# Adding the attention mask on VectorE in nine of twelve groups, with other steps and orders re-assigned, in a two-layer attention trunk

## The chip, the cores and the metric

The kernel runs on one core of a Trainium2 chip. The metric is the time of one execution on the device in microseconds (us); the median of the runs shown is compared. In the text PE is TensorE (matmuls and transposes, with PEld for its weight loads), DVE is VectorE, ACT is ScalarE, POOL is GpSimd, SP is the engine whose queue issues the DMAs. L353 is line 353 of the kernel before; the change moves most lines of the changed kernel one to twelve further down, so that its names are given where its lines are meant.

## The reference, cut to what matters

Two layers over 256 tokens of width 1024, 16 heads of 64. Layer 0 attends over a sliding window of 128 tokens with a learned sink a head, in 2 key heads; layer 1 is block-sparse attention which, at 256 tokens and a block of 256, is plain causal attention, in 4 key heads. Both gate the attention output by silu(z) and add an output projection to the residual; a last RMSNorm ends the trunk.

```python
for i in range(DEPTH):                       # DEPTH = 2
    hn = rmsnorm(h, norm_g[i])
    q, k, v, z = split_proj(hn, w_in, n_kv)  # one input projection
    q, k = apply_rope(q, cos, sin), apply_rope(k, cos, sin)
    # layer 0: softmax over [masked scores (128-token window), sink]
    # layer 1: softmax over causal scores
    o = attention(q, k, v)
    h = h + (o.reshape(B, S, MIX_WIDTH) * silu(z)) @ w_out[i]
return rmsnorm(h, final_g)
```

The mask is additive, 0 or -1e30, and the softmax subtracts the row's maximum (in layer 0 the larger of it and the sink) before the exponential.

## The kernel before, in words

**Weights.** Each layer's weights come from HBM in pieces of 128 x 1024 float32 (`load`). A piece is used in one of two ways. Most are split (`split`, L100 to L120): ACT writes a rounded high part `whi` (L113), DVE subtracts it from the piece to get the low part `wlo` (L114), and every block of the projection is then three matmuls, high by high, high by low and low by high (L150 to L152 with the activations' own halves, the `quad` tiles; L438 to L440 and L475 to L477 in the output projections). In the text such three matmuls are a triple. The pieces numbered in `NATIVE` are not split: one full float32 matmul of `xf` (L148), which the profile records as two matmuls. `PACE` makes the ACT part of each split wait for the DVE part of the split before it.

**Attention.** `attn(c, b, u, qs)` handles one group of heads for one block `b` of 128 queries. There are six groups a layer, called here (layer, c, b, u): for b = 0 one group of 8 heads over 128 keys, for b = 1 two groups (u = 0, 1) of 4 heads over 256 keys. A group goes as follows:

- PE: scores into the one tile `sc` in PSUM (`NSC` = 1), two banks, one for the even and one for the odd heads (L349); then two bf16 matmuls, one a bank, add the mask, an identity times the mask repeated for every head of the bank (L353; 512 columns, or 256 in layer 1 for b = 1, where half of the keys need no mask).
- DVE: one reduction over all 1024 score columns gives the negated maximum of each head, `nm` (L355); in layer 0 `nm` is then taken against the sink (L359) and `es` prepared (L360).
- ACT: an exponential a head from `sc` into `p`, with its sum in `rs` (L363); in layer 0 the sink's exponential `es` (L361), which DVE adds to `rs` (L365).
- DVE: the reciprocal `ri` (L366); then a scaling of `p` a head, by ACT (L369) for groups in the table `PSC`, else by DVE (L371).
- PE: eight transposes (L377) into two `tr` tiles; each copied to a `pT` tile (`NPT` of them) by DVE (L380) for groups in `PEV`, else by ACT (L382).
- PE: the product with the values into `o` (L392); DVE multiplies by the gate `sz` (L398), ACT takes the high part (L404), POOL (groups in `GLP`) or DVE the low part (L405).

**Other work that tables place.** `RPL`: which rotary halves (L242, L243) go to POOL instead of DVE. `SZP`: which gate tiles (L423 to L426) go to POOL. `SQP`: which squares of the residual for the norm go to POOL (L175) instead of ACT (L177). `NACC`: into how many tiles the squares are summed; the norm's sum over the partitions is then one matmul a tile and token block (L189).

**Order.** PE is fed by a scheduler that orders the instructions of each engine at build time from the priorities `PRI0` and `PRI1` and its own estimate of times; on the chip each engine then runs its list strictly in that order. `ORDERS` sets in which order the three groups of a half c come. Between the scores and the transposes of a group other matmuls (projections, earlier groups) are placed, so that the softmax of the group can run meanwhile on DVE and ACT.

**End.** `outp_r(1, True)` makes the last rows, 128 tokens at a time (t = 0, 1): matmuls, the residual add (L479), the sum of squares by ACT for the first 512 columns (L483) and by a two-input multiply-and-reduce on DVE for the rest (L486), the power on POOL (L492), and the scaling by norm and weight: POOL multiplies two of the four quarters by the weight ahead (L489) and ACT scales them (L495), DVE does the other two in one step each (L496). For t = 1 each of the four quarters is one DMA (L500).

Of the kernel before, what the change touches and what calls it, by code (L numbers as in the profile page):

```python
# [26 lines left out]
PSC = [(0, 0, 0, 0), (0, 0, 0, 1), (0, 0, 1, 1), (0, 1, 0, 1), (1, 0, 1, 0), (1, 0, 1, 1), (1, 1, 0, 0), (1, 1, 1, 0)]
PEV = [(0, 0, 0, 0), (0, 0, 1, 0), (0, 1, 0, 0), (0, 1, 0, 1), (0, 1, 1, 0), (0, 1, 1, 1), (1, 0, 0, 0), (1, 0, 1, 0), (1, 1, 0, 0), (1, 1, 0, 1), (1, 1, 1, 0)]
NRAW, NHI, NLO = 10, 7, 5
PRI0 = {'xf': -162.8, 'hi': -265.1, 'sr': -286.8, 'tr': -272.9, 'skv': 98.1, 'st': -212.1, 'kv': -263.2, 'sq0': 99.4, 'q0': 98.9, 'sz0': 45.8, 'z0': 45.7, 'a0': -114.0, 'sq1': -459.0, 'q1': -26.7, 'a1': -421.4, 'sz1': -118.7, 'z1': 71.8, 'so0': -61.1, 'o0': -294.2, 'so1': 9.0, 'o1': -290.0, 'r0': -69.2, 'r1': -190.1, 'rk': -186.0, 'p0': -402.1, 'p1': -134.3, 'e0': 48.7, 'e1': -109.7, 'f0': -206.4, 'f1': 27.1}  # L30
# [14 lines left out]
def trunk(ctx: ExitStack, tc: tile.TileContext, xT, gf, sinks, consts, masks, wkva, w, out):  # L45
# [161 lines left out]
    for layer in range(2):  # L207
# [122 lines left out]
        def attn(c, b, u, qs):  # L330
# [31 lines left out]
            for n in range(nh):  # L362
                nc.scalar.activation(p[:, n], sc[:, n % 2, n // 2], AF.Exp, bias=nm[:, n:n + 1], accum_out=rs[:, n:n + 1])  # L363
# [226 lines left out]
```

## Time and profile before

| | |
|---|---|
| three runs | 222.77, 222.79, 223.54 us, median 222.79 |
| the profiled execution's own time | 223.15 us |
| its span, first to last instruction | 221.3 us |
| granted TensorE clock, mean | 0.989 |
| PE busy | 212.5 us, 1535 matmuls |
| DVE busy | 157.6 us |
| ACT busy | 128.7 us |
| POOL busy | 63.5 us |

How to read it: the span is 1.85 us shorter than the profiled execution's time, and that execution is 0.36 us over the median. The end of a matmul is modelled in the profile, so that overlapping matmuls in a row show as one unbroken stretch; how long one takes out of PE's stream is read from the distance between starts. In a row of the timeline a group of equal instructions is merged, with the start of the first, the time to the end of the last, and their number behind the x.

### The profile page before, as it was taken

What the parts mean: (1) busy time and instruction counts of PE and PEld (TensorE: products, weight loads), DVE (VectorE), ACT (ScalarE), POOL (GpSimd) and SP (SyncE); (2) the same over time, 40 slices, a digit from 0 to 9 for tenths busy, and PEclk for the clock granted to TensorE, in tenths of its full rate; (3) what the DMA queues carried; (4) which work ended last, traced back from release to release, by engine and by line L of the source; (5) the groups of instructions that cost most, each with busy time, mean ns of one, the idle gap of its engine ahead of it and who ended that gap; (6) DMA issues with size and microseconds to landing.
All of it is one profiled execution on the core that took longest, in us unless ns stands there. A gap on an engine that the chain in (4) does not pass through costs nothing.

```text
span 221.3 us, 4120 instructions
## 1 busy us (share of the span) xinstructions
PE 212.5 (96%) x1535; PEld 185.9 (84%) x1535; DVE 157.6 (71%) x291; ACT 128.7 (58%) x323; POOL 63.5 (29%) x69
## 2 busy tenths in 40 slices
PE   8989999999999999999999999999999999999970
PEld 4879999986989778989999999999799987668870
DVE  2458767858777769958975586889637799577471
ACT  7593355785469445327971555383967985843121
POOL 2562960220241712013631362320620011011231
PEclk9999999999999999999999999999999999999995
DMA  5899998535152323354534476654410000000022
GB/s 172 280 400 412 405 392 288 167 143 169 44 170 77 115 64 129 95 175 123 172 115 142 156 244 182 186 193 129 114 76 3 1 4 0 0 0 3 0 95 95
DMA packets 10532, 31.71 MB, mean 143 GB/s; under 512 B 1296, under 2 KB 2704, under 8 KB 10512
## 3 DMA queue, kind: packets, MB, share of 16 engines
q1 hardware_dynamic: 10512, 31.45, 42.7%
q8 instruction: 12, 0.20, 0.4%
q14 instruction: 8, 0.07, 0.1%
HBM read 30.39 MB, written 1.05 MB: 142 GB/s over the span
## 4 chain that ended last, share of the span: by engine, by line
PE 88%; ACT 3%; DMA 3%; SPq 2%; DVE 1%; issue 1%; POOL 0%; POOLq 0%; ACTq 0%
PE mm L152 12%; PE mm L151 11%; PE mm L150 11%; PE mm L148 9%; PE sc L349 6%; PE o L392 6%; PE tr L377 5%; PE mm L438 4%; PE mm L439 4%; PE mm L440 3%; PE mm L477 3%; PE mm L475 3%; PE mm L476 3%; DMA hg<-xT 3%; PE sc L353 3%; SPq L95 1%
## 5 line engine op out<-in xcount | busy, mean ns | idle before, releaser
L114 DVE TENSOR_TENSOR wlo<-wraw,whi 128x1024 fp32r<-128x1024 f32 (+2 forms) x48 | 60.2, 1257 | 19.3 <-ACT whi L113 15.0
L113 ACT ACTIVATE whi<-wraw 128x1024 fp32r<-128x1024 f32 (+2 forms) x48 | 48.7, 1025 | 40.2 <-DVE wlo L114 29.9
L150 PE MATMUL mm<-quad,whi 128*128 128x256 f32 x216 | 64.0, 298 | 0.1
L152 PE MATMUL mm<-quad,wlo 128*128 128x256 f32 x216 | 62.0, 289 | 0.1
L151 PE MATMUL mm<-quad,whi 128*128 128x256 f32 x216 | 61.5, 286 | 0.0
L150 PEld LDWEIGHTS mm<-quad,whi 128*128 128x128 f32 x216 | 41.3, 192 | 1.1 <-ACT whi L113 0.6
L151 PEld LDWEIGHTS mm<-quad,whi 128*128 128x128 f32 x216 | 41.4, 191 | 1.0 <-issue 0.4
L152 PEld LDWEIGHTS mm<-quad,wlo 128*128 128x128 f32 x216 | 41.0, 191 | 0.8 <-DVE wlo L114 0.3
L363 ACT ACTIVATE p<-sc,nm 128x128 f32<-128x128 f32 (+1 forms) x64 | 26.0, 425 | 15.9 <-DVE nm L359 9.1
L148 PE MATMUL mm<-xf,wraw 128*128 128x256 f32 x112 | 26.9, 380 | 0.7 <-ACT xf L168 0.7
L148 PEld LDWEIGHTS mm<-xf,wraw 128*128 128x128 f32 x112 | 20.2, 190 | 3.4 <-ACT xf L168 1.1
L423 POOL TENSOR_TENSOR th<-th,z 128x256 f32<-128x256 f32 x9 | 8.7, 967 | 42.8 <-ACT th L421 42.6
L355 DVE TENSOR_REDUCE nm<-sc 128x4 f32<-128x1024 f32 (+1 forms) x12 | 14.6, 1220 | 7.2 <-PE sc L353 7.2
L242 POOL TENSOR_TENSOR t<-t,csr 128x512 f32<-128x512 f32 (+1 forms) x7 | 11.4, 1624 | 26.0 <-DVE t L238 18.9
L405 POOL TENSOR_TENSOR quad<-gf,quad 128x256 fp32r<-128x256 f32 x7 | 5.2, 742 | 46.5 <-ACT quad L404 46.5
L438 PE MATMUL mm<-quad,whi 128*128 128x256 f32 x64 | 18.3, 291 | 0.0
L439 PE MATMUL mm<-quad,whi 128*128 128x256 f32 x64 | 18.2, 285 | 0.0
L440 PE MATMUL mm<-quad,wlo 128*128 128x256 f32 x64 | 18.0, 282 | 0.0
L170 DVE SCALAR_TENSOR_TENSOR quad<-hg,quad 128x256 fp32r<-128x256 f32 x16 | 11.1, 702 | 7.1 <-ACT quad L169 7.1
L349 PE MATMUL sc<-ks,qs 64*128 64x128 f32 (+1 forms) x128 | 15.2, 348 | 0.0
L377 PE MATMUL tr<-cst,p 128*128 128x128 f32 x96 | 14.6, 275 | 0.0
L180 POOL TENSOR_TENSOR sq<-sq 128x256 f32<-128x256 f32 x14 | 11.9, 849 | 6.8 <-ACT sq L177 6.0
(105 smaller groups left out, 387.8 us busy)
## 6 DMA issues: line engine op xcount, KB each, us to landing
wraw<-w SPq DMA_DIRECT2D x50, 512.0 KB, 4.8
wraw<-wkva SPq DMA_DIRECT2D x2, 512.0 KB, 8.6
wraw<-w SPq DMA_DIRECT2D x3, 256.0 KB, 4.2
hg<-xT SPq DMA_DIRECT2D x2, 256.0 KB, 6.4
wraw<-gf SPq DMA_DIRECT2D x1, 512.0 KB, 3.5
out<-of SPq DMA_DIRECT2D x2, 256.0 KB, 2.2
out<-of SPq DMA_DIRECT2D x4, 128.0 KB, 1.9
hg<-xT SPq DMA_DIRECT2D x3, 128.0 KB, 3.5
```

Source lines behind the costliest of these rows:

```text
L113: ia = nc.scalar.activation(a[:, c0:c1], r[:, c0:c1], AF.Copy)
L114: ib = nc.vector.tensor_sub(b[:, c0:c1], r[:, c0:c1], a[:, c0:c1].bitcast(F32))
L148: nc.tensor.matmul(ps, wh, x, start=start, stop=stop)
L150: nc.tensor.matmul(ps, wh, xh, start=start, stop=False)
L151: nc.tensor.matmul(ps, wh, xl, start=False, stop=False)
L152: nc.tensor.matmul(ps, wl, xh, start=False, stop=stop)
L349: nc.tensor.matmul(sc[:, par, i], qs[half, 2 * us[0] + i, b * P:(b + 1) * P], ks[half, (h0 + n) // per, :nk], start=i == 0, stop=False)
L363: nc.scalar.activation(p[:, n], sc[:, n % 2, n // 2], AF.Exp, bias=nm[:, n:n + 1], accum_out=rs[:, n:n + 1])
L377: nc.tensor.transpose(pt[:, n], p[:, n0 + n, kt * P:(kt + 1) * P], ident)
L438: nc.tensor.matmul(ps, wh, gh, start=k == 0, stop=False)
L439: nc.tensor.matmul(ps, wh, gl, start=False, stop=False)
L440: nc.tensor.matmul(ps, wl, gh, start=False, stop=k == 3)
```

## The change

1. Nine of the twelve groups, those in the new table `TTM`, get no mask matmuls. For each of their heads one DVE instruction reads the scores from PSUM and the mask from SBUF, adds them, writes the negated sum to `p` and reduces it with a minimum to `nm`. In layer 0 it starts from the negated sink, so that L359 falls away. It replaces the reduction over the whole group; the instruction is followed by a short one that writes its accumulator out. The exponential then reads `p` instead of `sc` and takes the scale -1, and in these groups `sc` is free after DVE's last head instead of after ACT's. The three groups left as they were are (0, 0, 0, 0), (1, 0, 1, 0) and (1, 1, 1, 0).
2. The last rows: POOL multiplies the first 512 columns by the weight in one step while the second 512 are still in work; ACT scales that half in one instruction, DVE the other half in one, and each half is one DMA, for t = 1 too.
3. Tables: pieces 9 and 17 are split instead of native and piece 10 native instead of split; layer 0 runs two rotary halves more on DVE; scaling moves from DVE to ACT in three groups of four heads; the copies of three groups of layer 0 move from DVE to ACT, and of one group of layer 1, on balance, to DVE; three more squares go to POOL; the squares are summed in two tiles a layer instead of one; six `pT` tiles instead of three; a different order of groups in layer 0, and all priorities.

```diff
-NATIVE = (1, 2, 5, 6, 9, 13, 17, 31)
-RPL = [(0, 'k'), (0, 0, 0), (0, 0, 1), (0, 1, 1), (1, 'k'), (1, 0, 0), (1, 1, 0)]
+NATIVE = (1, 2, 5, 6, 10, 13, 31)
+RPL = [(0, 'k'), (0, 0, 0), (1, 'k'), (1, 0, 0), (1, 1, 0)]
...
-PSC = [(0, 0, 0, 0), (0, 0, 0, 1), (0, 0, 1, 1), (0, 1, 0, 1), (1, 0, 1, 0), (1, 0, 1, 1), (1, 1, 0, 0), (1, 1, 1, 0)]
+PSC = [(0, 0, 0, 0), (0, 0, 0, 1), (0, 0, 1, 0), (0, 0, 1, 1), (0, 1, 1, 1), (1, 0, 1, 0), (1, 0, 1, 1), (1, 1, 0, 0), (1, 1, 1, 0), (1, 1, 1, 1)]
...
-NRAW, NHI, NLO = 10, 7, 5
+NRAW, NHI, NLO = 10, 6, 5
-NPT = 3
+NPT = 6
-ORDERS = [[[(0, 0), (1, 0), (1, 1)], [(0, 0), (1, 0), (1, 1)]], [[(0, 0), (1, 1), (1, 0)], [(0, 0), (1, 1), (1, 0)]]]
+ORDERS = [[[(1, 0), (0, 0), (1, 1)], [(1, 0), (0, 0), (1, 1)]], [[(0, 0), (1, 1), (1, 0)], [(0, 0), (1, 1), (1, 0)]]]
+TTM = [(0, 0, 1, 0), (0, 0, 1, 1), (0, 1, 0, 0), (0, 1, 1, 0), (0, 1, 1, 1), (1, 0, 0, 0), (1, 0, 1, 1), (1, 1, 0, 0), (1, 1, 1, 1)]
-SQP = [(0, 0), (0, 2), (0, 4), (1, 0)]
-NACC = [1, 1]
+SQP = [(0, 0), (0, 1), (0, 3), (0, 5), (1, 1), (1, 5), (1, 6)]
+NACC = [2, 2]
...
+            wide = (layer, c, b, u) in TTM
             for n in range(nh):
...
                 nc.tensor.matmul(sc[:, par, i], qs[half, 2 * us[0] + i, b * P:(b + 1) * P],
-                                 ks[half, (h0 + n) // per, :nk], start=i == 0, stop=False)
-            k0 = nk - P if layer else 0
-            for par in range(2):
-                nc.tensor.matmul(sc[:, par, :, k0:], mkb[:, 0], mask[:, None, k0:].to_broadcast([P, np_, nk - k0]),
-                                 start=False, stop=True)
-            nc.vector.tensor_reduce(nm.rearrange("p (i r) -> p r i", r=2), sc, axis=mybir.AxisListType.X, op=OP.max,
-                                    negate=True)
+                                 ks[half, (h0 + n) // per, :nk], start=i == 0, stop=wide and i == np_ - 1)
+            if wide:
+                for n in range(nh):
+                    nc.vector.tensor_tensor_reduce(out=p[:, n], in0=sc[:, n % 2, n // 2], in1=mask, scale=-1.0,
+                                                   scalar=3.0e38 if layer else nsink[:, h0 + n:h0 + n + 1],
+                                                   op0=OP.add, op1=OP.min, accum_out=nm[:, n:n + 1])
+            else:
...
             for n in range(nh):
-                nc.scalar.activation(p[:, n], sc[:, n % 2, n // 2], AF.Exp, bias=nm[:, n:n + 1], accum_out=rs[:, n:n + 1])
+                if wide:
+                    nc.scalar.activation(p[:, n], p[:, n], AF.Exp, bias=nm[:, n:n + 1], scale=-1.0, accum_out=rs[:, n:n + 1])
+                else:
+                    nc.scalar.activation(p[:, n], sc[:, n % 2, n // 2], AF.Exp, bias=nm[:, n:n + 1], accum_out=rs[:, n:n + 1])
...
-                            if c0 % 512 == 0:
-                                nc.gpsimd.tensor_mul(hf[:, c0 // 512], hv[:, :2], gk[:, c0 // P:c0 // P + 2])
+                            if c0 == 0:
+                                nc.gpsimd.tensor_mul(hf, hv, gk[:, :4])
...
+                        nc.scalar.activation(o[:, :4], hf, AF.Copy, scale=ms[:, 1:])
+                        nc.vector.scalar_tensor_tensor(o[:, 4:], h[:, 4:, tok], ms[:, 1:], gk[:, 4:], op0=OP.mult, op1=OP.mult)
                         for i in range(2):
-                            nc.scalar.activation(o[:, 4 * i:4 * i + 2], hf[:, i], AF.Copy, scale=ms[:, 1:])
-                            nc.vector.scalar_tensor_tensor(o[:, 4 * i + 2:4 * i + 4], h[:, 4 * i + 2:4 * i + 4, tok],
-                                                           ms[:, 1:], gk[:, 4 * i + 2:4 * i + 4], op0=OP.mult, op1=OP.mult)
-                            for j in (range(2) if t else (0,)):
-                                k0, k1 = (4 * i + 2 * j, 4 * i + 2 * j + 2) if t else (4 * i, 4 * i + 4)
-                                nc.sync.dma_start(out[tok, k0 * P:k1 * P], o[:, k0:k1].rearrange("p k s -> p (k s)"))
+                            nc.sync.dma_start(out[tok, 512 * i:512 * i + 512],
+                                              o[:, 4 * i:4 * i + 4].rearrange("p k s -> p (k s)"))
```

What the tables do to the order is shown at one place on two engines, the group (0, 1, 1, 0): second half of layer 0, second query block, first four heads. The rows are of the lists that each engine runs; `mm`, `sc`, `tr` and `o` are PSUM tiles, `quad` and `xf` activations, a row with x8 is eight equal instructions, and a native matmul (of `xf`), a score or a product `o` counts once where the profile records two.

PE before, from the scores of that group to the next matmuls behind them:

```order
321 L349 MATMUL sc<-ks,qs 128x256 x4
322 L353 LDWEIGHTS mkb
323 L353 MATMUL sc<-mkb 128x512
324 L353 LDWEIGHTS mkb
325 L353 MATMUL sc<-mkb 128x512
326 L377 MATMUL tr<-cst,p 128x128 x8
327 L438 MATMUL mm<-quad,whi 128x256
```

PE now, from the same scores on (the transposes in row 248 are those of the group ahead, (0, 0, 1, 1)):

```order
244 L351 MATMUL sc<-ks,qs 128x256 x4
245 L404 MATMUL o<-pT,vs 64x256 x4
246 L153 MATMUL mm<-quad,wlo 128x256
247 L149 MATMUL mm<-xf,wraw 128x256 x3
248 L389 MATMUL tr<-cst,p 128x128 x8
249 L149 MATMUL mm<-xf,wraw 128x256
250 L151 MATMUL mm<-quad,whi 128x256
```

The two mask matmuls and their weight loads are gone, and the group stands earlier, inside the gate projection. Before, its own transposes come in row 362, between them 8 transposes, 27 matmuls of triples, 4 native ones, 8 products `o` and 4 heads of the next scores with their masks. Now they begin in row 267, behind the rows shown, five more matmuls of triples, the eight heads of scores of (0, 1, 0, 0) in row 256 and ten matmuls of triples.

DVE before, from the reduction of that group to its neighbours' work:

```order
79 L355 TENSOR_REDUCE nm<-sc 128x2x2
80 L380 COPY pT<-tr 128x512
81 L359 TENSOR_TENSOR nm<-nm,nsink 128x4
82 L360 TENSOR_TENSOR es<-nm,sink 128x4
83 L380 COPY pT<-tr 128x512
84 L398 TENSOR_TENSOR gf<-o,sz 128x256
85 L365 TENSOR_TENSOR rs<-rs,es 128x4
86 L366 RECIPROCAL ri<-rs 128x4
```

DVE now, from the last of the four heads (an instruction of the reduce kind is listed as ISA, its accumulator's read in the row behind it) to the scaling:

```order
80 L355 ISA p,nm<-sc,mkb,nsink 128x256
81 L355 ISA nm 128x1
82 L115 TENSOR_TENSOR wlo<-wraw,whi 128x1024
83 L369 TENSOR_TENSOR es<-nm,sink 128x4
84 L432 TENSOR_TENSOR z<-mm,rh 128x256
85 L377 TENSOR_TENSOR rs<-rs,es 128x4
86 L378 RECIPROCAL ri<-rs 128x4
87 L383 TENSOR_SCALAR p<-p,ri 128x256 x4
```

Four pairs (rows 74 to 81) stand where one reduction and L359 stood, with nothing between them, and a weight split now lies between them and the group's `es`. On ACT the four exponentials, then the next split's `whi`, then the `es` of this group follow each other.

More of the change, by code (lines that the diff above doesn't have):

```diff
@@ L349, in attn @@
                 nc.tensor.matmul(sc[:, par, i], qs[half, 2 * us[0] + i, b * P:(b + 1) * P],
-                                 ks[half, (h0 + n) // per, :nk], start=i == 0, stop=False)
-            k0 = nk - P if layer else 0
-            for par in range(2):
-                nc.tensor.matmul(sc[:, par, :, k0:], mkb[:, 0], mask[:, None, k0:].to_broadcast([P, np_, nk - k0]),
-                                 start=False, stop=True)
-            nc.vector.tensor_reduce(nm.rearrange("p (i r) -> p r i", r=2), sc, axis=mybir.AxisListType.X, op=OP.max,
-                                    negate=True)
+                                 ks[half, (h0 + n) // per, :nk], start=i == 0, stop=wide and i == np_ - 1)
[5 more added lines that the diff above has]
+            else:
+                k0 = nk - P if layer else 0
+                for par in range(2):
+                    nc.tensor.matmul(sc[:, par, :, k0:], mkb[:, 0], mask[:, None, k0:].to_broadcast([P, np_, nk - k0]),
+                                     start=False, stop=True)
+                nc.vector.tensor_reduce(nm.rearrange("p (i r) -> p r i", r=2), sc, axis=mybir.AxisListType.X, op=OP.max,
+                                        negate=True)
             if layer == 0:
                 es = work.tile([P, 8], F32, name="es", bufs=4)[:, :nh]
-                nc.vector.tensor_tensor(nm, nm, nsink[:, h0:h0 + nh], op=OP.min)
+                if not wide:
+                    nc.vector.tensor_tensor(nm, nm, nsink[:, h0:h0 + nh], op=OP.min)
                 nc.vector.tensor_add(es, nm, sink[:, h0:h0 + nh])
@@ L467, in outp_r @@
                     if final:
-                        hf = act.tile([P, 2, 2, P], F32, name="hf", tag="quad", bufs=6)
+                        hf = act.tile([P, 4, P], F32, name="hf", tag="quad", bufs=6)
                         gk = gfin.rearrange("p (k s) -> p k s", s=P)
```

10 lines of the change are left out of this document (5 added, 5 removed).

## The prediction

> **What bounds the kernel now.** I read the page first: busy times, then the shares of the chain that ended last.
>
> ```profile
> span 221.3 us, 4120 instructions
> PE 212.5 (96%) x1535; PEld 185.9 (84%) x1535; DVE 157.6 (71%) x291; ACT 128.7 (58%) x323; POOL 63.5 (29%) x69
> ...
> PE 88%; ACT 3%; DMA 3%; SPq 2%; DVE 1%; issue 1%; POOL 0%; POOLq 0%; ACTq 0%
> ```
>
> PE is on the chain for 88% of the span. Whether DVE has room for more work has to be read by stage, so the second view is the busy time by stretches (columns: stretch, its length, then PE, PEld, DVE, ACT and POOL).
>
> ```profile
> 16.20:88.00 71.80, 71.68 (x522) 61.70 (x523) 54.85 (x117) 41.47 (x120) 23.34 (x22) 1.00 0.57 201
> 120.00:200.00 80.00, 80.00 (x614) 69.90 (x613) 60.15 (x97) 52.70 (x133) 19.53 (x17) 1.00 0.30 93
> 215.00:221.30 6.30, 0.00 (x0) 0.00 (x0) 1.70 (x7) 0.91 (x2) 0.56 (x1) 0.62 0.25 83
> ```
>
> The first two hold the attention of layer 0 and of layer 1. PE has no free time there, at a granted clock of 1.00; DVE is busy 76% and 75%, ACT 58% and 66%. So what leaves PE's stream shortens the kernel, and what is added to DVE costs nothing as long as PE does not come to wait for it. The last stretch is PE-free: 6.3 us of norm, scaling and output, all on the path.
>
> **The PE terms.** Mask matmuls first, by the distance of starts in PE's timeline: the wide pair of layer 1's first group, the narrow pair, and scores with no mask behind them (half a group, followed by other work).
>
> ```profile
> 135.72 0.39 PE L152 MATMUL mm<-quad,wlo 128*128 128x256 f32 x1
> 135.94 0.28 PE L150 MATMUL mm<-quad,whi 128*128 128x256 f32 x1
> ...
> 141.59 0.60 PE L353 MATMUL sc<-mkb 128*128 128x512 bf16 x2
> 142.16 0.28 PE L150 MATMUL mm<-quad,whi 128*128 128x256 f32 x1
> 142.28 0.28 PE L151 MATMUL mm<-quad,whi 128*128 128x256 f32 x1
> ...
> 150.74 0.39 PE L353 MATMUL sc<-mkb 128*128 128x256 bf16 x2
> 151.09 0.28 PE L150 MATMUL mm<-quad,whi 128*128 128x256 f32 x1
> ```
>
> Without masks the second matmul behind the scores starts 0.22 us after the first. With a wide pair it starts 0.57 after the pair's start, with a narrow one 0.35. The pairs cost 0.35 and 0.13. Seven of the nine groups have wide pairs (five of layer 0, two of 8 heads in layer 1), two have narrow ones: 7 x 0.35 + 2 x 0.13 = 2.7 us less. The chain books more on them, which is my upper end:
>
> ```profile
> 36.23 1.73 PE mm L148 x8
> 62.69 1.09 PE sc L349 x16
> 73.99 0.87 PE tr L377 x8
> 76.29 1.01 PE o L392 x8
> 120.51 0.34 PE tr L189 x4
> 141.66 0.54 PE sc L353 x2
> 150.81 0.33 PE sc L353 x2
> ```
>
> By its 0.54 and 0.33 it is 7 x 0.54 + 2 x 0.33 = 4.4 us. I take 2.7, because the chain counts to modelled ends and starts are recorded.
>
> One native piece fewer: 8 full matmuls are 16 records, two rows like the 1.73, 3.46 us; as triples they are 24 x 0.12 (142.16 to 142.28) = 2.88 us. 0.6 us less. Squares summed in two tiles: 8 more of L189, at 0.34 / 4 = 0.085, 0.7 us more. PE in sum: -2.7 - 0.6 + 0.7 = -2.6 us. The instructions that only change their place on PE keep their cost.
>
> **What DVE and ACT get.** The rows of the groups by line and shape (busy us, mean ns, idle before); of the multiply-and-reduce kind before has only three, in the last rows.
>
> ```profile
> L114 DVE TENSOR_TENSOR wlo<-wraw,whi 128x1024 fp32r<-128x1024 f32 x45 | 58.8, 1306 | 18.7 <-ACT whi L113 14.4 <-PE mm L152 3.0 <-PE mm L440 0.9
> L113 ACT ACTIVATE whi<-wraw 128x1024 fp32r<-128x1024 f32 x45 | 47.3, 1062 | 40.0 <-DVE wlo L114 29.9 <-DMA wraw<-w 4.0 <-PE tr L377 2.2
> L380 DVE COPY pT<-tr 128x512 f32<-128x512 f32 x18 | 12.0, 683 | 1.9 <-PE o L392 1.9
> L355 DVE TENSOR_REDUCE nm<-sc 128x4 f32<-128x1024 f32 x8 | 9.8, 1222 | 6.5 <-PE sc L353 6.5
> L420 DVE TENSOR_TENSOR z<-mm,rh 128x256 f32<-128x256 f32 x16 | 6.5, 414 | 0.9 <-PE mm L152 0.6 <-PE mm L148 0.3
> L371 DVE TENSOR_SCALAR p<-p,ri 128x256 f32<-128x256 f32 x16 | 4.7, 347 | 0.1
> L242 DVE TENSOR_TENSOR t<-t,csr 128x512 f32<-128x512 f32 x3 | 2.0, 668 | 0.0
> L366 DVE RECIPROCAL ri<-rs 128x4 f32<-128x4 f32 x8 | 1.4, 174 | 2.7 <-ACT p L363 2.5
> L361 ACT ACTIVATE es<-es 128x4 f32<-128x4 f32 x4 | 0.8, 209 | 0.0
> L479 DVE TENSOR_TENSOR hg<-hg,mm 128x128 f32<-128x128 f32 x1 | 0.3, 277 | 0.0
> ```
>
> And the end, in the timeline (start, length):
>
> ```profile
> 212.64 0.74 POOL L489 TENSOR_TENSOR hf<-hg,wraw 128x256 f32<-128x256 f32 x1 [1.59 <-DVE hg L479]
> ...
> 214.06 1.19 DVE L486 CUSTOM_DVE_ANT_1 t<-hg,st 128x384 f32<-128x384 f32 x1
> 214.10 0.73 POOL L489 TENSOR_TENSOR hf<-hg,wraw 128x256 f32<-128x256 f32 x1 [0.72 <-DVE hg L479]
> 215.49 0.35 DVE L486 CUSTOM_DVE_ANT_0 t<-hg,st 128x128 f32<-128x128 f32 x1
> 216.52 0.91 ACT L495 ACTIVATE of<-hf,ms 128x256 f32<-128x256 f32 x2 [3.15 <-POOL ms L492]
> 216.52 0.88 DVE L496 SCALAR_TENSOR_TENSOR of<-hg,ms,wraw 128x256 f32<-128x256 f32 x2 [0.67 <-POOL ms L492]
> 217.03 1.80 SPq L500 DMA_DIRECT2D out<-of  x4
> ```
>
> The price of the new instruction is the main unknown. At 128 columns the kind takes 0.35 us, 0.075 over an add of that size (0.277). An add of 256 columns that reads PSUM takes 0.414, so 0.49 is my value for 256 columns. The 1.19 us at 384 is out of line by 0.56 (by the same slope, 0.0011 us a column, it should be 0.63). I put that down to POOL, which runs L489 beside it and reads SBUF as it does; the 0.35 has no POOL step beside it. The upper end, if the 1.19 is the kind's own price, is 0.56 more for each. The lower end is the bare adds, 0.41 and 0.28. [...]
>
> DVE in layer 0: 16 x 0.49 + 8 x 0.35 = 10.6, less 5 reductions of 1.22 and the five L359, each taken as 0.2 like the reciprocal: +3.5. Two rotary halves of two steps, 4 x 0.67: +2.7. One split: +1.3. Eight scalings of 0.347: -2.8. Six copies of 0.683: -4.1. In sum +0.6, 55.5 us in a stretch that shrinks to about 70: 79%. Layer 1: 16 x 0.35 + 8 x 0.49 - 4 x 1.22 = +4.6, two copies +1.4, four scalings -1.4; the moved gate steps are under 1 us and go off DVE: 64.8 of about 79, 82%. ACT takes the scalings and copies of layer 0, at about DVE's own times 7 us, and one split: 50 of 70. All of it lies beside PE, at nought; with the cover gone it costs what the rivals below do.
>
> Whether a group's softmax still fits is seen at its shortest distance on PE, the group (0, 1, 1, 0), whose rows stand above. Between its scores and its transposes lie 8 records of `o` (1.01), 17 matmuls of triples (2.04), 4 native ones (1.73), 8 transposes (0.87) and 8 heads of scores (1.09): 6.7 us. Its way needs four pairs (2.0), then, since `es` stands behind a split on ACT and that waits for the split on DVE, 1.31 + 1.06, `es` 0.21, the sum and the reciprocal 0.17 each, and the first scaling 0.35: 5.3. About 1.4 us are left. The other groups have 8.7 us or more by the same count.
>
> **The end.** POOL now multiplies 512 columns from 212.64 on, some 1.5 us, to 214.1; the reduction at 214.06 is free of it: 1.19 to 0.63, of which 0.5 reach the path, since the add behind it began 0.07 early. Bounds 0 (POOL not the cause) and 0.56. Then two halves instead of four quarters. An instruction of twice the size I put at 0.75, between one and two (0.88, 0.91). The last of four issues starts 1.35 after 217.03, at 218.4; now the last of two starts at 216.52 + 0.75 + 0.45 = 217.7: 0.7 less. Larger DMAs land later:
>
> ```profile
> out<-of SPq DMA_DIRECT2D x2, 256.0 KB, 2.2
> out<-of SPq DMA_DIRECT2D x4, 128.0 KB, 1.9
> ```
>
> 0.3 of it is given back. The end in sum: -0.5 - 0.4 = -0.9 us, within -1.3 and 0.
>
> **Sum.** 223.15 - 2.6 - 0.9 = 219.65 us against the profiled execution's own time. That is 0.36 over the median, so the forecast is 219.3 us, 1.6% less. About 0.5% (1.1 us) is what a measurement of this kernel can tell from no change; 221.7 and 223.9 are those bounds.
>
> **The rivals.**
>
> *The masks cost what the chain says.* Then 1.7 us more go: 217.6. For it: the bf16 pair loads its own weights. Against: the starts. 0.12.
>
> *PE waits in layer 0.* Each row of the new order was set by estimated times, and a group reaches PE late if DVE starts its pairs late by over 1.4 us. A reduction of 1024 columns in 1.22 becomes 2.0 in four pieces and 2.8 in eight, so each group's first reader on ACT starts earlier but its last later. If three of the six groups of layer 0 wait 0.9 us each, 2.7 comes back: 222.0. For it: DVE's row L114 shows 18.7 us of idle time waiting for ACT, which 79% busy does not remove. Against: no wait of PE's shows before, at 76%. 0.22. [...]
>
> *Slower: the new instruction costs as the 1.19 row does*, 1.05 us at 256 columns and 0.91 at 128, with or without POOL. DVE then gets 24 x 0.56 = 13.4 us more in each layer: 69 of 70 and 78 of 79, no room. At the shortest distance a group of four comes 4 x 0.56 - 1.4 = 0.8 us late, one of eight, with 2.5 us more distance, 0.6: 6 x 0.8 + 3 x 0.6 = 6.6, 225.9. It decides from 0.49 + 1.4 / 4 = 0.84 us a pair of 256 columns on. For it: two of three rows of the kind are slow. Against: both have a POOL step beside them. 0.10.
>
> **How the numbers follow.** My forecast has 0.50, the rivals 0.12, 0.22 and 0.10; 0.06 is left for a wait elsewhere, above 223. Faster by over 0.5%: 0.50 + 0.12 + 0.10 of the 0.22 (shorter waits), 0.72. Within: the other 0.12 and 0.02 of the rest, 0.14. Slower: 0.14. The range goes from 217.4, under the chain's price, to 222.6, above the waits in layer 0; what it leaves out is the slow price and the rest.
>
> **What would show it.** PE's matmuls 1533, with 6 masks instead of 24; PE's busy time down by some 3 us. The new instruction at 0.49 and 0.35; DVE busy about 162 us. No idle time of PE in front of transposes or `o` in layer 0. From PE's last matmul to the end 6 us instead of 7. A price above 0.84, PE waiting on ACT or DVE in the groups of layer 0, or the stretch to 16 us longer would make it wrong.

## The result, and the profile after

The changed kernel takes 219.46 us (219.22 to 219.63), the kernel before 222.78: a ratio of 0.984 with a 95% interval of 0.982 to 0.986, so 3.2 to 3.9 us less. The forecast was 219.3.

The profiled execution took 219.47 us. The head of its page and the shares of the chain:

```profile
span 217.7 us, 4176 instructions
PE 210.3 (97%) x1533; PEld 185.4 (85%) x1533; DVE 156.0 (72%) x359; ACT 137.8 (63%) x335; POOL 59.5 (27%) x67
...
PE 89%; DMA 2%; SPq 2%; DVE 2%; issue 1%; ACT 1%; POOL 1%; POOLq 0%
```

PE has 1533 matmuls and 2.2 us less busy time, and DVE with 68 more instructions is busy 1.6 us less, not 4 more. The busy time by stretches (stretch, its length, then PE, PEld, DVE, ACT, POOL), cut where the attention of layer 0, that of layer 1 and the end lie now:

```profile
16.20:86.00 69.80, 69.80 (x525) 61.52 (x525) 56.74 (x152) 49.94 (x135) 16.98 (x18) 1.00 0.58 204
118.00:197.00 79.00, 79.00 (x604) 70.14 (x605) 61.05 (x136) 54.32 (x135) 21.40 (x20) 1.00 0.30 94
211.50:217.70 6.20, 0.47 (x5) 0.32 (x3) 1.83 (x6) 0.72 (x1) 0.56 (x1) 0.90 0.23 85
```

PE fills both attention stretches again, at a clock of 1.00; DVE is busy 81% and 77% there. PE's own waits over the whole span are three (who waits, for whom; us in total, times, longest), none of them inside the softmax of a group:

```profile
PE mm L75 <- DVE mhalf L138: 1.0, 1, 1.0
PE mm L151 <- ACT whi L114: 0.4, 1, 0.4
PE mm L149 <- ACT xf L169: 0.3, 1, 0.3
```

The groups by line and shape (busy us, mean ns of one) show what the new instruction costs, by column count and layer (those with `nsink` are layer 0), the reads of its accumulator behind it, what remains of masks, and the reductions of the last rows:

```profile
L355 DVE CUSTOM_DVE_ANT_0 p<-sc,mkb,nsink 128x256 f32<-128x256 f32 x16 | 6.8, 475 | 2.6 <-PE sc L351 2.6
L355 DVE DVE_READ_ACCUMULATOR2_ANT nm<- 128x1 f32 x48 | 4.0, 83 | 0.0
L355 DVE CUSTOM_DVE_ANT_0 p<-sc,mkb 128x128 f32<-128x128 f32 x16 | 3.6, 285 | 2.3 <-PE sc L351 2.3
L355 DVE CUSTOM_DVE_ANT_0 p<-sc,mkb 128x256 f32<-128x256 f32 x8 | 2.9, 420 | 0.0
L355 DVE CUSTOM_DVE_ANT_0 p<-sc,mkb,nsink 128x128 f32<-128x128 f32 x8 | 2.2, 346 | 0.0
L361 PE MATMUL sc<-mkb 128*128 128x256 bf16 x4 | 0.8, 278 | 0.0
L498 DVE CUSTOM_DVE_ANT_1 t<-hg,st 128x512 f32<-128x512 f32 x1 | 0.7, 743 | 0.0
L498 DVE CUSTOM_DVE_ANT_1 t<-hg,st 128x384 f32<-128x384 f32 x1 | 0.6, 618 | 0.0
L361 PE MATMUL sc<-mkb 128*128 128x512 bf16 x2 | 0.6, 384 | 0.0
```

The same masks and reductions in the kernel before:

```profile
L353 PE MATMUL sc<-mkb 128*128 128x512 bf16 x16 | 4.8, 384 | 0.0
L353 PE MATMUL sc<-mkb 128*128 128x256 bf16 x8 | 1.6, 278 | 0.0
L486 DVE CUSTOM_DVE_ANT_1 t<-hg,st 128x512 f32<-128x512 f32 x1 | 1.3, 1329 | 0.0
L486 DVE CUSTOM_DVE_ANT_1 t<-hg,st 128x384 f32<-128x384 f32 x1 | 1.2, 1185 | 0.0
```

And the end in the timeline (start, length):

```profile
209.47 1.30 POOL L501 TENSOR_TENSOR hf<-hg,wraw 128x512 f32<-128x512 f32 x1 [1.46 <-DVE hg L491]
...
211.30 0.62 DVE L498 CUSTOM_DVE_ANT_1 t<-hg,st 128x384 f32<-128x384 f32 x1
...
211.69 0.28 PE L489 MATMUL mm<-whi,quad 128*128 128x128 f32 x1
...
212.77 0.56 POOL L504 TENSOR_TENSOR ms<-st,mhalf 128x1 f32<-128x1 f32 x1 [2.00 <-DVE st L498]
213.36 0.72 ACT L506 ACTIVATE of<-hf,ms 128x512 f32<-128x512 f32 x1 [3.15 <-POOL ms L504]
213.36 0.75 DVE L507 SCALAR_TENSOR_TENSOR of<-hg,ms,wraw 128x512 f32<-128x512 f32 x1 [0.67 <-POOL ms L504]
```

POOL is done with L501 at 210.77, half a microsecond ahead of the reduction, which takes 0.62 where it took 1.19. From PE's last start (211.69) to the end of the span (217.69) it is 6.00 us; before it was 7.19 (214.15 to 221.34).

**Where the time went.** To see which part of PE's stream shrank, I took the start of each of its matmuls in the two traces and added up, by kind, the distance to the next start. A matmul that waits is thus booked on the one ahead of it. The triples are those with an activation of 256 tokens; those of the very last projection (L475 to L477 before) are in the row of the rest. (us, number in brackets)

```
kind                      before        after        difference
masks                      2.82 (24)     0.63 (6)     -2.19
native pieces             27.15 (128)   23.20 (112)   -3.95
triples                  117.21 (912)  120.68 (936)   +3.47
sums of squares            0.73 (8)      1.62 (16)    +0.89
transposes of p            9.27 (96)     8.18 (96)    -1.09
scores, o, all the rest   55.99         56.40         +0.41
sum to the last start    213.17        210.71         -2.46
from there to the end      7.19          6.00         -1.19
```

The two terms together are 3.65 us, the difference of the spans.

Two rows are booked with a neighbour and have to be read together with it. Behind a pair of masks the triple's first matmul takes 0.31 us (wide) or 0.20 (narrow), where it takes 0.22 behind scores without masks: about 0.5 us that left with six wide pairs stands in the triples' row. And a transpose holds PE for 0.11 us with another transpose behind it, but for 0.03 with a triple behind it, which then takes 0.20 instead of 0.12. Now 31 transposes have a triple behind them, before 19 had. So about 1.0 us moved from the transposes' row into that of the triples, and it is no gain.

### The profile page after: what moved, and what is told of

Same layout as the page of the kernel before. It is cut to its first block, busy times and chain, and to the rows that moved or that the text cites. A ratio compares the mean times of both kernels' runs of the same rounds, so it can differ in the third digit from the quotient of the medians.

```text
span 217.7 us, 4176 instructions
## 1 busy us (share of the span) xinstructions
PE 210.3 (97%) x1533; PEld 185.4 (85%) x1533; DVE 156.0 (72%) x359; ACT 137.8 (63%) x335; POOL 59.5 (27%) x67
## 3 DMA queue, kind: packets, MB, share of 16 engines
HBM read 30.39 MB, written 1.05 MB: 144 GB/s over the span
## 4 chain that ended last, share of the span: by engine, by line
PE 89%; DMA 2%; SPq 2%; DVE 2%; issue 1%; ACT 1%; POOL 1%; POOLq 0%
PE mm L151 13%; PE mm L153 12%; PE mm L152 12%; PE mm L149 9%; PE sc L351 6%; PE o L404 6%; PE tr L389 5%; PE mm L451 4%; PE mm L452 4%; PE mm L450 4%; PE mm L487 3%; PE mm L489 3%; PE mm L488 2%; DMA hg<-xT 2%; SPq L96 1%
## 5 line engine op out<-in xcount | busy, mean ns | idle before, releaser
L114 ACT ACTIVATE whi<-wraw 128x1024 fp32r<-128x1024 f32 (+2 forms) x49 | 49.6, 1021 | 38.8 <-DVE wlo L115 18.3
L151 PE MATMUL mm<-quad,whi 128*128 128x256 f32 x224 | 66.4, 298 | 0.4 <-ACT whi L114 0.4
L152 PE MATMUL mm<-quad,whi 128*128 128x256 f32 x224 | 64.4, 288 | 0.0
L151 PEld LDWEIGHTS mm<-quad,whi 128*128 128x128 f32 x224 | 42.8, 191 | 2.3 <-issue 1.1
L152 PEld LDWEIGHTS mm<-quad,whi 128*128 128x128 f32 x224 | 42.8, 191 | 0.7
L373 ACT ACTIVATE p<-p,nm 128x256 f32<-128x256 f32 (+1 forms) x48 | 21.3, 444 | 5.0 <-DVE nm L355 4.9
L149 PE MATMUL mm<-xf,wraw 128*128 128x256 f32 x96 | 23.3, 380 | 0.3 <-ACT xf L169 0.3
L149 PEld LDWEIGHTS mm<-xf,wraw 128*128 128x128 f32 x96 | 17.3, 190 | 2.5 <-ACT xf L169 0.6
L451 PE MATMUL mm<-quad,whi 128*128 128x256 f32 x64 | 18.3, 286 | 0.0
L450 PE MATMUL mm<-quad,whi 128*128 128x256 f32 x64 | 18.3, 286 | 0.0
L381 ACT ACTIVATE p<-p,ri 128x256 f32<-128x256 f32 (+1 forms) x44 | 16.8, 458 | 1.4 <-DVE ri L378 1.3
L351 PE MATMUL sc<-ks,qs 64*128 64x256 f32 (+1 forms) x128 | 15.2, 348 | 0.0
L487 PE MATMUL mm<-whi,quad 128*128 128x512 f32 (+2 forms) x36 | 13.9, 385 | 0.0
L404 PE MATMUL o<-pT,vs 128*64 128x256 f32 x96 | 13.7, 395 | 0.0
L488 PE MATMUL mm<-wlo,quad 128*128 128x512 f32 (+2 forms) x36 | 13.3, 373 | 0.0
```

Source lines behind the costliest of these rows:

```text
L114: ia = nc.scalar.activation(a[:, c0:c1], r[:, c0:c1], AF.Copy)
L149: nc.tensor.matmul(ps, wh, x, start=start, stop=stop)
L151: nc.tensor.matmul(ps, wh, xh, start=start, stop=False)
L152: nc.tensor.matmul(ps, wh, xl, start=False, stop=False)
L351: nc.tensor.matmul(sc[:, par, i], qs[half, 2 * us[0] + i, b * P:(b + 1) * P], ks[half, (h0 + n) // per, :nk], start=i == 0, stop=wide and ...
L404: im = nc.tensor.matmul(po[64 * par:64 * par + 64, i0:i0 + 2], vs[:, kt, (h0 + 2 * i0) // per], pTs[j][:, par::2], start=st, stop=sp)
```

## The experiments

Each kernel ran in five rounds beside the kernel before; a ratio is to that. In most of them the scheduler built the order of all engines anew, as it does for any kernel whose instructions change; three kept the order, and where that matters it is said.

**Each half of the change by itself.** First only the end (the lines of the diff from `hf` on), in the kernel before; PE's order stays the same:

```diff
-                        hf = act.tile([P, 2, 2, P], F32, name="hf", tag="quad", bufs=6)
+                        hf = act.tile([P, 4, P], F32, name="hf", tag="quad", bufs=6)
...
-                            if c0 % 512 == 0:
+                            if c0 == 0:
```

> The kernel before with the new end alone: 512 columns weighted by POOL in one step ahead, halves scaled by one engine each, two DMAs for the last rows. Theory: the reduction of 384 columns falls from 1.19 to about 0.62 us, 0.9 us less in all, 221.9. Rival (the end gives nothing by itself, all came from PE): 222.8.

Measured 221.57 us, ratio 0.994 (0.993 to 0.995): 1.4 us less, between 1.1 and 1.7. The same rows of the end in its timeline:

```profile
211.86 1.30 POOL L489 TENSOR_TENSOR hf<-hg,wraw 128x512 f32<-128x512 f32 x1 [1.46 <-DVE hg L479]
...
213.69 0.62 DVE L486 CUSTOM_DVE_ANT_1 t<-hg,st 128x384 f32<-128x384 f32 x1
...
214.08 0.28 PE L477 MATMUL mm<-whi,quad 128*128 128x128 f32 x1
...
215.75 0.75 DVE L495 SCALAR_TENSOR_TENSOR of<-hg,ms,wraw 128x512 f32<-128x512 f32 x1 [0.67 <-POOL ms L492]
```

The reduction falls from 1.19 to 0.62, and PE's last start is 6.00 us from the end, as in the changed kernel. The end is a part of its own and brings the same alone or with the rest.

Then only the nine groups, with the tables and the end of before:

```diff
+TTM = [(0, 0, 1, 0), (0, 0, 1, 1), (0, 1, 0, 0), (0, 1, 1, 0), (0, 1, 1, 1), (1, 0, 0, 0), (1, 0, 1, 1), (1, 1, 0, 0), (1, 1, 1, 1)]
...
+            if wide:
+                for n in range(nh):
+                    nc.vector.tensor_tensor_reduce(out=p[:, n], in0=sc[:, n % 2, n // 2], in1=mask, scale=-1.0,
...
```

> The kernel before with the nine groups masked and reduced by DVE, and all other tables and the end as before. Theory (only PE's stream counts, DVE has room): 2.7 us less, 220.1, no idle time of PE. Rival (the tables that take scalings and copies off DVE are what makes it fit): PE waits in the groups of layer 0 and a good part is given back, 221.3 or more.

Measured 221.62 us, ratio 0.994 (0.993 to 0.996): 1.3 us less, where 2.7 us of masks were to go. PE's stream shrinks by 1.5 us and has waits that neither kernel has:

```profile
PE tr L389 <- DVE pT L392: 0.4, 1, 0.4
PE mm L153 <- DVE wlo L115: 0.3, 1, 0.3
PE tr L466 <- ACT hg L467: 0.3, 1, 0.3
```

So half of what the masks were to free is lost while the tables stay as they were. The two halves make 2.7 us of the 3.2 to 3.9, each with 0.3 us of uncertainty; what is left for the new tables, if the parts add up, is about half a microsecond to one.

**What a mask costs.** The first attempt takes all 24 masks out of the kernel before (the mask is left out) and lets the order be built anew:

```diff
-            for par in range(2):
-                nc.tensor.matmul(sc[:, par, :, k0:], mkb[:, 0], mask[:, None, k0:].to_broadcast([P, np_, nk - k0]),
-                                 start=False, stop=True)
```

> The kernel before with its 24 mask matmuls left out, and nothing in their place, so that the mask is missing from the scores in all twelve groups. It measures what the masks cost PE by themselves. Theory (price by the distance of starts, 0.35 a wide pair and 0.13 a narrow one): 8 x 0.35 + 4 x 0.13 = 3.3 us less, 219.5. Rival (price as the chain books it, 0.54 and 0.33): 8 x 0.54 + 4 x 0.33 = 5.6 us less, 217.2.

Measured 225.18 us, ratio 1.012 (1.009 to 1.015): slower, with less to do. Both forecasts missed. Its PE waits where the kernel before never does:

```profile
PE tr L373 <- ACT p L365: 0.9, 1, 0.9
PE tr L450 <- DVE pT L376: 0.7, 1, 0.7
PE mm L150 <- DVE z L416: 0.6, 1, 0.6
```

By the same sum of starts its products `o` take 3.0 us more and its transposes 2.0 more than before. The 24 matmuls are gone, and the order that the scheduler built without them loses more than they cost. This run says nothing on their price. The second attempt therefore keeps the order: the kernel before is built as it is, and every other mask is cut out of the finished list of instructions, so that DVE, ACT, POOL and SP run the same lists as before and PE the same but for 12 matmuls and as many weight loads. (The scores of the unmasked rows end their sum themselves, by `stop`.)

```diff
+    for f in nc.m.functions:
+        for b in f.blocks:
+            kept, masks = [], 0
+            for i in b.instructions:
+                if type(i).__name__ in ("InstMatmult", "InstLdweights") and any("memref='mkb" in str(a) for a in i.ins):
+                    masks += 1
+                    if masks % 4 in (2, 3):
+                        continue
+                kept.append(i)
+            b.instructions = kept
```

> The kernel before, with every other one of its 24 mask matmuls cut out of the finished program (in each group the first row of scores stays unmasked), so that the order of all other instructions on all engines stays what it was. It tells the price of a mask matmul apart from the order that a scheduler rebuilds. Removed: 8 of 512 columns, 4 of 256. By the prediction's prices (0.35 us a wide pair, 0.13 a narrow one) 8 x 0.175 + 4 x 0.065 = 1.66 us, so 221.1 us beside 222.8. By the starts of TensorE's matmuls in the trace of before (24 masks hold 2.82 us, 0.118 each) 1.4 us, so 221.4. By the chain's price (0.54 and 0.33 a pair) 8 x 0.27 + 4 x 0.165 = 2.8 us, so 220.0. If the masks only fill time in which TensorE would have waited for something else, as the kernel without masks might be read, no change: 222.8.

Measured 221.18 us, ratio 0.992 (0.989 to 0.995): 1.8 us less, between 1.2 and 2.4. What is left of masks in its groups:

```profile
L353 PE MATMUL sc<-mkb 128*128 128x512 bf16 x8 | 3.1, 389 | 0.0
L353 PE MATMUL sc<-mkb 128*128 128x256 bf16 x4 | 1.1, 283 | 0.0
```

PE's stream is 1.6 us shorter. The expectation gave 1.66 by the prediction's prices and 2.8 by the chain's, and 2.8 lies outside the interval.

The starts show how a pair is paid. In the kernel before, a wide pair with a triple behind it (seven of eight) has the distances 0.226 (first mask), 0.029 (second mask) and 0.308 us (the triple's first matmul); without masks that first matmul takes 0.22. The pair thus costs 0.34. A narrow pair has 0.120, 0.029 and 0.201, and costs 0.13. These are the prediction's 0.35 and 0.13, at every such place, and a quarter of the wide price stands behind the masks, not in them. A mask that stands alone holds PE for 0.04 us, and the triple behind it still takes 0.31. So to cut one of two frees more than half, 0.22 and 0.11, or 2.2 us for the 12. PE's stream got 1.6 of it: the transposes of the group (0, 0, 0, 0) take 0.45 us more, since they now wait for ACT's scaling, behind which they already stood by only 0.06 us before. That the time came out near the expected 1.66 is luck: halving the price of a pair was too little, and the wait made up for it.

**The kernel after without its nine groups** (all twelve groups mask on PE; the new tables and the end stay):

```diff
-TTM = [(0, 0, 1, 0), (0, 0, 1, 1), (0, 1, 0, 0), (0, 1, 1, 0), (0, 1, 1, 1), (1, 0, 0, 0), (1, 0, 1, 1), (1, 1, 0, 0), (1, 1, 1, 1)]
+TTM = []
```

> The changed kernel with no group in the new table, so that all twelve have mask matmuls and the one reduction again, with the new end and the other new tables. Theory: 2.7 us more than the changed kernel, 222.2. Rival (the new order and the other tables brought the gain): within 1 us of the changed kernel, under 220.5.

Measured 224.95 us, ratio to the kernel before 1.010 (1.008 to 1.012), so 5.5 us over the kernel after instead of 2.7. The masks hold PE for 3.5 us, 2.9 more than after; `o` and the transposes take 2.4 more; and a wait is new:

```profile
PE mm L450 <- ACT quad L416: 1.0, 1, 1.0
```

The tables of after are made for the nine groups: without those they are worse than the tables of before, as the tables of before are worse with them.

**All twelve groups.**

```diff
-TTM = [(0, 0, 1, 0), (0, 0, 1, 1), (0, 1, 0, 0), (0, 1, 1, 0), (0, 1, 1, 1), (1, 0, 0, 0), (1, 0, 1, 1), (1, 1, 0, 0), (1, 1, 1, 1)]
+TTM = [(l, c, b, u) for l in range(2) for c in range(2) for b, u in ((0, 0), (1, 0), (1, 1))]
```

> The changed kernel with all twelve groups masked and reduced by DVE. Theory: one wide pair and two narrow ones less on PE, 0.35 + 0.26 = 0.6 us less than the changed kernel, 218.9. Rival (DVE at 81% in layer 0 has no room left, so that these three were left out with reason): PE waits, 219.5 or more.

Measured 220.64 us, ratio 0.990 (0.988 to 0.991): 1.2 us over the kernel after, with no mask left on PE. Again a wait of PE's that the order built for nine groups doesn't have:

```profile
PE mm L151 <- DVE z L432: 1.1, 1, 1.1
```

DVE's busy time is 157.8 us there, 1.8 over after. The last three groups would free 0.6 us on PE by the sum of starts; the wait takes more.

**The two terms that PE gets beside the masks.** Squares in one tile again:

```diff
-NACC = [2, 2]
+NACC = [1, 1]
```

> The changed kernel with the squares of each layer summed into one tile again. Theory: eight matmuls of 0.085 less on PE, 0.7 us less, 218.8. Rival (the sum over the partitions comes later, since POOL adds one after the other, and PE or DVE waits for the norm): 219.5 or more.

Measured 219.09 us, ratio 0.983 (0.981 to 0.985). The sums of squares take 0.73 us of PE's starts instead of 1.62, so 0.9 less where 0.7 was priced, but the times of this kernel and the kernel after overlap (218.93 to 219.91, and 219.22 to 219.63). Then the list of native pieces of before:

```diff
-NATIVE = (1, 2, 5, 6, 10, 13, 31)
+NATIVE = (1, 2, 5, 6, 9, 13, 17, 31)
```

> The changed kernel with the old list of unsplit pieces, eight instead of seven. Theory: 0.6 us more on PE, 220.1. Rival (a split less on DVE and ACT is worth as much): 219.5.

Measured 219.31 us, ratio 0.984 (0.982 to 0.985): no difference to the kernel after. In the sum of starts native pieces are 3.36 up and triples 3.08 down, a cost of 0.3 us by these two rows, half of the 0.6 of the prediction, but the triples' row changes with what stands ahead of them, as said above. In the time no cost is seen. Both together:

```diff
-NACC = [2, 2]
+NACC = [1, 1]
...
-NATIVE = (1, 2, 5, 6, 10, 13, 31)
+NATIVE = (1, 2, 5, 6, 9, 13, 17, 31)
```

> The kernel after, with the list of native matmul pieces of before and the squares in one tile again (NACC = [1, 1]). Each alone came out at 219.31 and 219.09 beside 219.46. If what each brings adds up (-0.15 and -0.37): 218.9, and the squares alone remove 0.9 us of TensorE's stream. Rival: the order that the scheduler builds anew is worth more than either, and it lands anywhere within a microsecond of 219.5, waits of TensorE inside the attention showing up that after does not have.

Measured 219.42 us, ratio 0.983 (0.981 to 0.986): the same as the kernel after (219.46), though 0.9 us of sums of squares are gone from PE again. What each seemed to bring alone doesn't add up. No kernel that I ran is faster than the kernel after by more than the runs scatter.

**Why the reduction of the last rows was slow.** In the kernel after, POOL is given a multiplication nobody reads, on 256 columns, at the place where before had L489. The orders of PE, ACT and DVE stay as they are.

```diff
                             if c0 == 0:
                                 nc.gpsimd.tensor_mul(hf, hv, gk[:, :4])
+                            elif c0 == 512:
+                                hx = work.tile([P, S], F32, name="th").rearrange("p (k s) -> p k s", s=P)
+                                nc.gpsimd.tensor_mul(hx, hv[:, :2], gk[:, 4:6])
```

> The changed kernel with one more POOL multiply of 256 columns, whose result nothing reads, as soon as the second half of the last rows is added, that is beside the reduction. Theory (POOL slows a reduction with two SBUF inputs): the reductions of 512 and 384 columns go from 0.74 and 0.62 back to about 1.3 and 1.2 us, and the end is 0.5 us longer, 220.0. Rival (they were faster for another reason): 0.74 and 0.62 stay, 219.5.

Measured 220.26 us (219.26 to 220.73), ratio 0.987 (0.985 to 0.989), 0.8 us over the kernel after. The profiled execution is the fastest of them, 219.26; its end is 6.42 us instead of 6.00, so that the trace shows half of the 0.8. The rows, first those of the first 128 tokens:

```profile
205.60 0.73 POOL L504 TENSOR_TENSOR th<-hg,wraw 128x256 f32<-128x256 f32 x1 [0.73 <-DVE hg L491]
205.97 0.91 DVE L498 CUSTOM_DVE_ANT_1 t<-hg,st 128x512 f32<-128x512 f32 x1
...
210.66 1.19 DVE L498 CUSTOM_DVE_ANT_1 t<-hg,st 128x384 f32<-128x384 f32 x1
210.70 0.73 POOL L504 TENSOR_TENSOR th<-hg,wraw 128x256 f32<-128x256 f32 x1 [0.43 <-DVE hg L491]
...
212.09 0.35 DVE L498 CUSTOM_DVE_ANT_0 t<-hg,st 128x128 f32<-128x128 f32 x1
```

The same instruction of 384 columns takes 1.19 us with POOL's multiplication beside it and 0.62 without; the one of 128 columns, with POOL idle, keeps its 0.35. So 0.57 us is what POOL beside it costs, and it isn't the instruction's own price. The one of 512 columns was expected at about 1.3 and took 0.91: POOL's step began 0.37 us ahead of it and ran beside it for 0.36 us only, and it is 0.17 longer than the 0.74 of the kernel after.

**How much more DVE could take.** In the kernel after, the new instruction is issued twice for every head, and in a second kernel for the first half of a group's heads only:

```diff
+                    for _ in range(2):
-                    nc.vector.tensor_tensor_reduce(out=p[:, n], in0=sc[:, n % 2, n // 2], in1=mask, scale=-1.0,
+                        nc.vector.tensor_tensor_reduce(out=p[:, n], in0=sc[:, n % 2, n // 2], in1=mask, scale=-1.0,
...
```

> The kernel after, with each of the 48 new instructions issued twice (the second repeats the first and gives the same values); the scheduler builds the order anew. VectorE's busy time rises by 16 x 0.475 + 8 x 0.42 + 8 x 0.346 + 16 x 0.285 = 18.3 us and the accumulator reads, to about 176 of 218. Theory (VectorE has room, and a group's way is hidden up to its margin, the tightest 1.4 us): each group's way grows by 1.7 to 2.5 us, which leaves 0 to 1 us past the margin of the tight groups: 219.5 to 222.5. Rival (the new instructions already stand in the path of most groups, and the gain is what is left after them): 9 groups times about 2 us, 230 us or more.

```diff
-                    for _ in range(2):
+                    for _ in range(2 if n < nh // 2 else 1):
```

> The kernel after, with the new instruction issued twice for the first half of each group's heads only: 24 more instructions, 8 x 0.475 + 4 x 0.42 + 4 x 0.346 + 8 x 0.285 = 9.1 us more on VectorE, 0.8 to 1.4 us more in the way of each of the nine groups, just inside the tightest margin of 1.4 us that the prediction counted. The order is built anew. If the margins are as the prediction counted them, the addition is hidden: 219.5, give or take the 1.5 us that orders built anew have come out from each other, so 218 to 221. If the 23 us of the whole doubling came in proportion (VectorE in the path of the groups already): 219.5 + 11.5 = 231. In between (222 to 228): the margins are there, but smaller than counted, and what exceeds them is paid with TensorE's waits and with the lower granted clock that follows them.

Measured 242.89 us, ratio 1.091 (1.087 to 1.094), and 228.81 us, ratio 1.027 (1.024 to 1.030): 23.4 and 9.3 us over the kernel after, for 19.3 and 10.5 us more of DVE. The first lands past its rival's 230, the second between its middle case (up to 228) and the proportional one (231); my theory that a group's margin hides the addition fell for these kernels. The granted clock was 0.957 over the profiled execution of the first and 0.993 over that of the second, beside 0.997 in the kernel after. The smaller one is 5.5 us behind the kernel after where layer 1's norm begins (129.9 and 124.4 us), and the other 4 come in layer 1. Its worst place in layer 0, by stretches (columns as above), and PE's longest waits:

```profile
84.00:90.00 6.00, 6.00 (x52) 5.73 (x49) 5.93 (x22) 1.75 (x4) 0.69 (x1) 1.00 0.13 45
90.00:96.00 6.00, 5.82 (x44) 4.58 (x43) 5.56 (x13) 3.32 (x10) 0.70 (x1) 1.00 0.50 166
96.00:102.00 6.00, 4.19 (x32) 3.21 (x32) 1.83 (x6) 2.79 (x6) 0.77 (x1) 1.00 0.29 93
```

```profile
PE mm L151 <- DVE z L433: 1.4, 1, 1.4
PE o L405 <- DVE pT L393: 1.4, 2, 0.7
PE mm L451 <- ACT quad L417: 1.0, 1, 1.0
PE mm L452 <- POOL quad L418: 1.0, 1, 1.0
```

DVE is busy 99% and 93% between 84 and 96 us, and then PE runs dry: this is the last group of layer 0, and PE's list has only output projections left beside it. The first of its scaled scores is ready at 98 us there, in the kernel after at 80. But this order was built anew for the longer instructions, and what part of the 9 us is DVE's and what part is the order can't be told from these two kernels. A version that keeps the order and only lengthens DVE's steps wasn't tried, so this stays open.

The margin of the kernel after itself can be read from its trace: for each group, the end of each scaling of `p` against the start of the transpose that reads it, the smallest difference of the group.

```
group          heads  margin us     group          heads  margin us
(0, 0, 1, 0)     4      2.09        (1, 0, 0, 0)     8      2.09
(0, 0, 0, 0)     8      3.19        (1, 0, 1, 1)     4      2.44
(0, 0, 1, 1)     4      2.60        (1, 0, 1, 0)     4      6.21
(0, 1, 1, 0)     4      1.81        (1, 1, 0, 0)     8      3.51
(0, 1, 0, 0)     8      1.36        (1, 1, 1, 1)     4      3.12
(0, 1, 1, 1)     4      2.49        (1, 1, 1, 0)     4      5.01
```

Every group is ahead of PE, by 1.4 us or more. (Against the weight load that reads `p` for the transpose it is 0.1 us less.) These are margins against one reader each; they don't say what DVE's other steps would do to each other if all groups grew at once.

## Why the prediction was right, step by step

- **What leaves PE's stream shortens the kernel, what DVE gets costs nothing under cover.** The first half held where the order was kept: 12 masks cut out gave 1.8 us in the time and 1.6 in the stream. It failed as a general rule: 24 masks taken out with a new order made the kernel 2.2 us slower. The second half held for this change (PE has no wait in a group, and the margins stand), and was too easy as a statement about DVE: with 10.5 us more in the same stretches, in an order built for it, 9.3 us came back.
- **The masks, -2.7 us.** By the starts they are 2.2 less in their own row and about 0.5 in the triples behind them, together 2.7. The two prices were read at one wide pair and one narrow one, and they hold at all others with a triple behind them, 0.34 and 0.13. The rival that the chain's 0.54 and 0.33 are the price is out: no pair costs that by its starts, and the 2.8 us that it gives for the 12 masks lies outside the measured 1.2 to 2.4.
- **One native piece fewer, -0.6.** Behind the first 18 us the native matmuls take 3.45 us less, the step's 3.46, and 24 matmuls of triples at 0.12 are its 2.9. So the price fits the starts; the time doesn't show it, since the kernel with the old list came out the same.
- **Squares in two tiles, +0.7.** +0.9 by the starts, and 0.9 back with one tile.
- **PE in sum -2.6.** Measured -2.46. The three terms came about as they stood. What no step had nearly cancels, and that is luck: the first 18 us of the span, where PE waits for what is loaded, are 0.6 us shorter after in these two executions (the 80th matmul starts at 17.6 instead of 18.2, and between 16.9 and 18.8 over all these kernels), which is not the change's, and the row of the rest is 0.4 longer.
- **The price of the new instruction, 0.49 and 0.35.** 0.475 and 0.346 in layer 0, where the lower bound comes from a tensor, 0.420 and 0.285 in layer 1, where it is a constant. The lower end of the step, the bare adds of 0.41 and 0.28, was the price in layer 1. DVE at 156.0 us instead of about 162: 24 instructions of each size make 15.5 us (6.8 + 2.9 + 2.2 + 3.6) where the step had 20.2. By their lengths they are 18.3, and where they stand in a row their records overlap: by their starts a head takes 0.40 and 0.27 in layer 0, 0.34 and 0.21 in layer 1, and the reads of the accumulator, which the step left out, lie in that time. Layer 1 came to 61.05 us where 64.8 stood. Layer 0 came to 56.7 of 69.8 (55.5 of about 70), ACT there to 49.9 (50).
- **The slow price as a rival** (1.05 us) is out: the longest of the 48 new instructions took 0.484, and the 1.19 behind it was POOL's, as the added multiplication showed. Its reckoning of 225.9 wasn't tested; going by the two kernels with repeated instructions, it would have been too low.
- **Waits of PE in layer 0 as a rival** didn't come. The group (0, 1, 1, 0), for which about 1.4 us were left, has 1.81. The tightest, though, is the one behind it, (0, 1, 0, 0) with 1.36, which the step had among those with much room: its distance is long, but so is the way of eight heads.
- **The end, -0.9.** -1.19. To the start of the last scaling 2.37 us became 1.67 (-0.70 where the step had -0.5): the reduction gave all of its 0.57. POOL's step of 512 columns took 1.30 us instead of the 1.5 that the step had, and was done half a microsecond ahead. From there to the end 4.82 became 4.33 (-0.49; the step had -0.4). The 0.75 us for an instruction of 512 columns was met: 0.72 and 0.75.

The profiled execution came 0.2 us under the sum of 219.65, the end 0.3 better and PE 0.1 worse. The forecast is all the same 0.2 under the median, since it took off the 0.36 us by which the profiled execution of before lies above its median, and that of after lies at it.

The low price held beside POOL too. The reduction of 384 columns, both of its inputs in SBUF, took 1.19 us beside POOL and 0.62 without. The new instruction, with one input in PSUM, took at most 0.01 us longer than its mean where POOL ran beside it for 0.2 us or more, as in 13 of the 48: 0.483 and 0.484 us in layer 0 at 256 columns beside 0.47 to 0.48 of most others, 0.28 to 0.29 in layer 1 at 128 with and without. No run shows why the two differ.

## What to carry to other kernels

Work taken off the bounding engine came near its price here while the order around it stayed (12 masks, 2.2 us by the starts: 1.8 us less), and not in every new order (all 24, priced at 3.3 us: 2.2 us more). Price it in a build that keeps the order, and read there too what comes back as a wait: of the seven kernels here with an order built anew, the two with repeated instructions aside, four came out 1 to 5.5 us worse than the price of the work that they added or left out, the other three within 0.8 of it, on either side. When a price is read from starts, look one instruction further, for part of it can stand behind the instruction that goes (0.09 of a wide pair's 0.34 us here). DVE, 81% and 77% busy beside a full PE, wasn't free for the rest (10.5 us more on it, in an order built for it, cost 9.3): read the margin of each group against its reader, and look at the places with little else to run, such as the last group of a layer, where PE ran dry in the kernel with half of the repeats. On a tail, look at what another engine does beside each slow instruction before taking its duration as its own (0.57 of the reduction's 1.19 us was POOL's).

## What the runs showed of the hardware

- With a lower bound from a [128, 1] tensor the add-and-reduce took 0.055 to 0.061 us longer than with a constant (475 and 420 ns at 256 columns, 346 and 285 at 128). A column costs 0.0010 to 0.0011 us in both. All instructions with the tensor are in layer 0 and all with the constant in layer 1; no run changes the bound alone, so it isn't shown that the bound is the cause.
- In the kernel with every instruction repeated, TensorE's clock fell twice ahead of PE's last matmul. PE's longest pause between two matmuls there was 2.23 us. Three stretches of its trace around the first fall (PEclk is the third number from the right):

```profile
93.00:96.00 3.00, 1.92 (x13) 0.91 (x12) 3.00 (x12) 0.73 (x3) 0.00 (x0) 1.00 0.16 61
96.00:99.00 3.00, 1.69 (x8) 1.44 (x7) 2.94 (x11) 1.76 (x7) 0.73 (x1) 0.64 0.00 0
99.00:102.00 3.00, 3.00 (x16) 3.00 (x15) 0.44 (x3) 2.33 (x7) 0.00 (x0) 0.50 0.01 3
```

PE is busy two thirds of the time from 93 to 96 us, and then full at a clock of 0.50: 16 matmuls in 3 us, where 23 to 28 ran in 3 us between 78 and 90. The clock is 0.50 from 96.8 to 103.7 us and again from 206.1 to 216.3. Over the whole kernel PE's busy time is 221.6 us for the 1533 matmuls that take 210.3 in the kernel after, so of the 22.5 us by which its span is longer some 11 are slower or held-up matmuls and 11 idle time. In the kernel with half the repeats PE was busy 4.19 of 6 us (96 to 102) and the clock stayed at 1.00. With every instruction repeated the pauses around the first fall are of 1.00, 1.08 and 1.31 us, with matmuls between them (from the ends and starts of PE's matmuls between 91 and 97.5 us), and the fall comes 0.7 us into the third; the second fall comes 0.8 us into the pause of 2.23 us. What brought the clock down these runs don't show.
